# A two-layer decoder trunk in split precision: the high and low part of the activations in one 512-wide product

## The chip, the cores and the metric

One core of a Trainium2 chip runs the whole trunk in one launch. The metric is the device time in microseconds (us) of the program, as the median of several runs. The engines are TensorE (PE, matrix products), VectorE (DVE), ScalarE (ACT), GpSimd (POOL) and SyncE (SP, which issues the transfers here).

## The reference

The input x has 256 positions of width 1024. Two layers follow each other; each computes, with `rms_norm` and three token mixers in parallel:

```python
z = rms_norm(x, mix_g)            # projected to 7960 columns: z, xbc, dt, rq, rk, rv, rg, gq, gk, gv, gr, gates
...
x = x + out(sum of gate_b * branch_b(mixer_b))      # Mamba-2 SSD, retention, gated linear attention
h = rms_norm(x, ffn_g)
u = causal_dwconv(h @ w_up, w, b)                   # 2 x 2816 columns, 3 taps over positions
x = x + (silu(u[..., :2816]) * u[..., 2816:]) @ w_down
```

A last `rms_norm` closes the trunk. Everything is float32.

## The kernel before, in words

A float32 operand is split into a high part in the reduced format fp32r, which PE multiplies, and a low part, the rest. A product is the sum of three: high by high, high by low, low by high. T is the 256 positions.

**Weights.** SP streams pieces of 128 x 1024 from HBM into `raw` (four buffers), ACT casts each to `whi` (L183), DVE subtracts to get `wlo` (L184); `piece()` asks for pieces five ahead of their use. There are 300 such casts on each engine, scattered through their queues.

**Activations.** Each of three `slots` holds a normalized or activated operand, transposed, as two tiles: `slot_h` (high) and `slot_l` (low), 128 x n x 256.

**Two kinds of product.** *Token-major* products (`tok_major`, L274 to L276) hold activations as the stationary operand and stream 512 weight columns; they need two accumulators, one per 128 positions. *Channel-major* products (`chan_steps`, L227 to L229) hold 128 weight columns and stream the 256 positions: for each of 8 row blocks k and 2 halves j three products of width 256, high by high, high by low, low by high, all into the same half of one accumulator. `chan_two` interleaves two such products, `chan_major` makes one. They are used for xbc (3 of them), rq, rk (2 each), gq, gk, and for the 22 column pairs of the up projection: 31 in a layer. `narrow` (L256, L260) is a short product for the small columns.

**PSUM.** `mm_tile` gives the accumulators of these products: 512 columns, one bank, four of them in rotation. `mx_tile` gives four more for everything else, among them the four sums of the down projection.

**Order at the start of a layer.** `chan_two` makes xbc 2 and xbc 0, then `chan_major` xbc 1, then comes the narrow group, then z, then two gates, then rq, rk and so on. As a channel product ends, its result goes to `take_xbc`: DVE multiplies it by the norm's factors `r_bc` into a `tm` tile (L459), ACT (L463) and DVE (six steps of L466) convolve it, ACT takes a tanh (L470), DVE multiplies (L471). `take_small` scales the narrow group's result (L475). `r_bc` itself comes at the end of `norm.factor` (a copy on ACT, L324). For the retention, a table `phases` is loaded over SP (L683) into `r_a` and multiplied by `r_bc` (L689).

**FFN.** `activate` takes an up product: DVE by `r_bc` (L1007), ACT and DVE convolve (L1012, L1014), ACT Silu (L1016), DVE multiplies the halves (L1017), ACT casts the high part (L1018), DVE makes the low part (L1019) in slot 2. `add_down` (L1024 to L1026) adds the down products of step j - 3 after the up product of step j; the last of them follow at the end.

Every engine takes its instructions in the order in which the program issues them; a scheduler of the framework sets that order when the program is built, and the waits between engines are fixed with it.

Of the kernel before, what the change touches and what calls it, by code (L numbers as in the profile page):

```python
# [17 lines left out]
P = 128  # L18
D = 1024
T = 256  # L20
# [107 lines left out]
def hybrid_trunk(ctx: ExitStack, tc: tile.TileContext, xT_in, x_in, wall, par, wa2, cst, phase, dret, fin, gbias, out):  # L128
# [27 lines left out]

    slots = []
    for i, n in enumerate((KT, KT, 4)):
        h = cpool.tile([P, n, T], F32R, name=f"slot_h{i}")
        lo = cpool.tile([P, n, T], F32R, name=f"slot_l{i}")  # L160
        slots.append((h, lo))


    loaded = {}
# [28 lines left out]
        return (a[:, c] for a in piece(p + o // step))  # L193

    def mm_tile():
        return ps.tile([P, 512], F32, name="mm", tag="mm", bufs=4)

    def mx_tile():
        return ps.tile([P, 512], F32, name="mx", tag="mx", bufs=4)
# [10 lines left out]
    def two(a):  # L210
        return a.rearrange("p (j t) -> p j t", j=2)
# [2 lines left out]
        return r_bc.unsqueeze(1).to_broadcast([P, 2, T])  # L214


    def chan_steps(l, kind, idx, act, acc, ks, nk=KT, cols=256, width=256, col0=0):

        ah, al = act
        nj = width // P  # L220
        for k in ks:
            wh, wl = weight(l, kind, idx, k, cols)
            for j in range(nj):
                c = slice(col0 + j * P, col0 + (j + 1) * P)
                o = acc[:, j * T:(j + 1) * T]
                first, last = k == 0 and j == 0, k == nk - 1 and j == nj - 1
                nc.tensor.matmul(o, lhsT=wh[:, c], rhs=ah[:, k, :], start=first, stop=False)  # L227
                nc.tensor.matmul(o, lhsT=wh[:, c], rhs=al[:, k, :], start=False, stop=False)  # L228
                nc.tensor.matmul(o, lhsT=wl[:, c], rhs=ah[:, k, :], start=False, stop=last)  # L229

    def chan_major(l, kind, idx, act, nk=KT, **more):
        acc = mm_tile()
        for k in range(0, nk, 2):
            chan_steps(l, kind, idx, act, acc, (k, k + 1), nk, **more)
            if k < nk - 2:
                yield
        return acc

    def chan_two(l, kind, idx, act, take):

        acc = [mm_tile() for _ in range(2)]
        for n in LATE:
            i, k = n // 8, n % 8
            chan_steps(l, kind, idx[i], act, acc[i], (k, k + 1))
            if k == KT - 2:
                take(idx[i], acc[i])
            yield

    def narrow(l, act):

        ah, al = act
        acc = mm_tile()
        both = piece(PIECE_AT[l, "small", 0][0])[0].rearrange("p (k c) -> p k c", c=P)
        for k in range(KT):
            def low():
                nc.tensor.matmul(acc[:64, :T], lhsT=both[:, k, :64], rhs=al[:, k, :], start=False, stop=False)  # L256

            if k == KT - 1:
                low()
            nc.tensor.matmul(acc[:, :T], lhsT=both[:, k, :], rhs=ah[:, k, :], start=(k == 0), stop=(k == KT - 1))  # L260
            if k < KT - 1:
                low()
        return acc

    def tok_major(l, kind, act, chunk=0, nk=KT):

        ah, al = act
        acc = [mm_tile() for _ in range(2)]
        for k in range(nk):
            wh, wl = weight(l, kind, chunk + k // 4, k % 4, 512)  # L270
            for t in range(2):
                c = slice(t * P, (t + 1) * P)
                first, last = k == 0, k == nk - 1
                nc.tensor.matmul(acc[t], lhsT=ah[:, k, c], rhs=wh, start=first, stop=False)  # L274
                nc.tensor.matmul(acc[t], lhsT=ah[:, k, c], rhs=wl, start=False, stop=False)  # L275
                nc.tensor.matmul(acc[t], lhsT=al[:, k, c], rhs=wh, start=False, stop=last)  # L276
            if k < nk - 1:
                yield
        return acc
# [150 lines left out]
    class Mixers:  # L430
# [3 lines left out]
        def __init__(self, l, norm):  # L434
            self.l, self.norm = l, norm
            self.pr = params[l]
            self.half = sm.tile([P, 30], F32, name="half", tag="half")
            nc.gpsimd.tensor_scalar(self.half[:, 0:30], self.pr[:, PO["conv_w"]:PO["conv_w"] + 30], 0.5, None,
                                    ALU.mult)
            self.aneg = sm.tile([P, 8], F32, name="aneg", tag="aneg")  # L440
            nc.scalar.activation(self.aneg, self.pc("a_log", 0, 8), AF.Exp)
            nc.vector.tensor_scalar(self.aneg, self.aneg, -1.0, None, ALU.mult)
            self.wa = mix.tile([P, T], F32, name="wa", tag="wa")
            nc.gpsimd.memset(self.wa, 0.0)
            for o in (32, 96):
                nc.sync.dma_start(self.wa[o:o + 16, :], wa2[l])
            y_h, y_l = slots[1]
            self.y_dst = [(y_h[:, 0:4, :], y_l[:, 0:4, :]), (y_h[:, 4:8, :], y_l[:, 4:8, :]), slots[2]]

        def pc(self, name, i=0, n=1):  # L450
            return self.pr[:, PO[name] + i:PO[name] + i + n]
# [2 lines left out]
        def take_xbc(self, b, acc):  # L454
            half = self.half
            if not hasattr(self, "xbc"):
                self.xbc = mix.tile([P, 6, T], F32, name="xbc", tag="g_work")
            ub = t_main()
            nc.vector.tensor_tensor(two(ub), two(acc), bc2(self.norm.r_bc), ALU.mult)  # L459
            for j in range(2):  # L460
                ct = 2 * b + j
                u, x = ub[:, j * T:(j + 1) * T], self.xbc[:, ct, :]
                nc.scalar.activation(x, u, AF.Identity, scale=half[:, 4 * ct + 3:4 * ct + 4],  # L463
                                     bias=half[:, 24 + ct:25 + ct])
                for d in (1, 2, 3):
                    nc.vector.scalar_tensor_tensor(x[:, d:], u[:, :T - d], half[:, 4 * ct + 3 - d:4 * ct + 4 - d],  # L466
                                                   x[:, d:], ALU.mult, ALU.add)
            th = t_main()
            xf = self.xbc[:, 2 * b:2 * b + 2, :]
            nc.scalar.activation(two(th), xf, AF.Tanh)  # L470
            nc.vector.scalar_tensor_tensor(xf, two(th), 1.0, xf, ALU.add, ALU.mult)  # L471
# [47 lines left out]
        def turn(self, h, wait):  # L519

            yield wait
            for q in (2 * h, 2 * h + 1):
                pt = mx_tile()
                for j in range(2):
                    for t in range(2):
                        c = (2 * q + j) * P
                        nc.tensor.transpose(pt[:, j * T + t * P:j * T + (t + 1) * P], self.merged[t][:, c:c + P], ident)
                mh, ml = (a[:, 2 * q:2 * q + 2, :].rearrange("p k t -> p (k t)") for a in slots[0])
                nc.scalar.activation(mh, pt, AF.Copy, scale=0.5)
                nc.vector.scalar_tensor_tensor(ml, pt, 0.5, mh.bitcast(F32), ALU.mult, ALU.subtract)  # L530
                yield 1


        def branch_operand(self, y, g, dst):

            h, lo = dst
            for c2 in range(2):
                pt = mx_tile()
                for j in range(2):
                    for t in range(2):  # L540
                        c = (2 * c2 + j) * P
                        nc.tensor.transpose(pt[:, j * T + t * P:j * T + (t + 1) * P], y[t][:, c:c + P], ident)  # L542
                for j in range(2):
                    ct = 2 * c2 + j
                    split_scaled(h[:, ct, :], lo[:, ct, :], pt[:, j * T:(j + 1) * T], self.pc(g, ct))
                yield 1
# [359 lines left out]
    def layer(l, norm):  # L906
# [92 lines left out]


        fx = slots[1]
        ah, al = slots[2]
        dacc = []

        def activate(j, acc):
            ub = t_main()
            nc.vector.tensor_tensor(two(ub), two(acc), bc2(norm.r_bc), ALU.mult)  # L1007
            cv = t_main()
            for i in range(2):
                ct = j + NF * i  # L1010
                u, a = ub[:, i * T:(i + 1) * T], cv[:, i * T:(i + 1) * T]
                nc.scalar.activation(a, u, AF.Identity, scale=mx.pc("fconv_w", 3 * ct + 2), bias=mx.pc("fconv_b", ct))  # L1012
                for d in (1, 2):
                    nc.vector.scalar_tensor_tensor(a[:, d:], u[:, :T - d], mx.pc("fconv_w", 3 * ct + 2 - d),  # L1014
                                                   a[:, d:], ALU.mult, ALU.add)
            nc.scalar.activation(cv[:, :T], cv[:, :T], AF.Silu)  # L1016
            nc.vector.tensor_tensor(cv[:, :T], cv[:, :T], cv[:, T:], ALU.mult)  # L1017
            nc.scalar.copy(ah[:, j % 4, :], cv[:, :T])  # L1018
            nc.vector.tensor_tensor(al[:, j % 4, :], cv[:, :T], ah[:, j % 4, :].bitcast(F32), ALU.subtract)  # L1019
# [186 lines left out]
```

## Time and profile before

| | |
|---|---|
| median of 3 runs | 933.4 us (932.29 to 935.02) |
| the profiled execution | 932.3 us, of which the span is 930.5 us |
| mean granted clock of PE | 0.994 of full speed |
| PE busy | 914.5 us (98%), 5726 products |
| DVE busy | 712.9 us (77%) |
| ACT busy | 506.8 us (54%) |
| mean traffic | 183 GB/s |

The span is the time between the first and the last recorded instruction; 1.8 us lie around it. Durations of PE's products overlap, since the next one enters the array before the last has left it; their starts are the better measure. A row that ends in a bracket tells how long its engine was idle before it, and which engine and line ended that.

### The profile page before, as it was taken

The page shows a single profiled execution, that of the slowest core. Times are in us where ns is not written, and L with a number is a line of the kernel's source. Part 1 is how long each engine was busy: PE and PEld are TensorE (multiplying, and loading weights), DVE is VectorE, ACT ScalarE, POOL GpSimd, SP SyncE. Part 2 cuts the span into 40 slices and gives each one's busy share as a digit, 9 for nine tenths or more (in the row PEclk, how much of TensorE's full clock was granted, in tenths as well). Part 3 has the DMA queues.
Part 4 walks back from the last instruction along what each step waited for, and adds up shares of the span by engine and source line. Part 5 has one row for each costly group of instructions (what it writes and reads, how often), then busy time and mean ns, then how long its engine had stood idle before and what let it go on. Part 6 is the DMA issues. An engine that isn't in the chain of part 4 may idle for free.

```text
span 930.5 us, 14996 instructions
## 1 busy us (share of the span) xinstructions
PE 914.5 (98%) x5726; PEld 816.1 (88%) x5726; DVE 712.9 (77%) x1111; ACT 506.8 (54%) x748; POOL 78.4 (8%) x74
## 2 busy tenths in 40 slices
PE   8999999999999999999999999999999999999995
PEld 7879889888889999999898898888888999999994
DVE  6976888576768887787799578777667697777775
ACT  6765454454456555555566635554545575555552
POOL 3032200003200000000002131000120000000001
PEclk9999999999999999999999999999999999999998
DMA  7775655556655656555466556444665566555531
GB/s 255 276 243 166 219 172 170 152 162 210 201 181 161 202 183 186 188 192 181 147 186 183 198 168 218 158 139 156 206 212 194 169 188 189 190 183 184 183 109 46
DMA packets 51288, 169.94 MB, mean 183 GB/s; under 512 B 5968, under 2 KB 8336, under 8 KB 51088
## 3 DMA queue, kind: packets, MB, share of 16 engines
q1 hardware_dynamic: 50928, 168.46, 56.3%
q8 instruction: 45, 0.74, 0.3%
q10 hardware_dynamic: 288, 0.52, 0.2%
q14 instruction: 27, 0.22, 0.1%
HBM read 165.81 MB, written 1.05 MB: 179 GB/s over the span
## 4 chain that ended last, share of the span: by engine, by line
PE 94%; DVE 3%; ACT 1%; DMA 1%; issue 0%; SPq 0%; ACTq 0%
PE mm L227 13%; PE mm L228 13%; PE mm L229 13%; PE mm L274 12%; PE mm L275 12%; PE mm L276 12%; PE mx L1025 4%; PE mx L1024 4%; PE mx L1026 4%; PE mx L555 2%; DVE wlo L184 1%; PE mx L558 1%; DVE xbc L466 1%; PE mx L542 1%; DMA x_t<-x_t 1%; PE mx L726 1%
## 5 line engine op out<-in xcount | busy, mean ns | idle before, releaser
L184 DVE TENSOR_TENSOR wlo<-raw,whi 128x1024 fp32r<-128x1024 f32 (+1 forms) x300 | 377.6, 1261 | 123.6 <-ACT whi L183 120.6
L183 ACT CAST whi<-raw 128x1024 fp32r<-128x1024 f32 (+1 forms) x302 | 311.7, 1034 | 266.4 <-PE mm L276 109.3
L227 PE MATMUL mm<-slot_h,whi 128*128 128x256 f32 x992 | 282.4, 285 | 2.2 <-ACT slot_h L302 2.2
L228 PE MATMUL mm<-slot_l,whi 128*128 128x256 f32 x992 | 281.5, 284 | 0.1
L229 PE MATMUL mm<-slot_h,wlo 128*128 128x256 f32 x992 | 281.5, 284 | 0.0
L274 PE MATMUL mm<-whi,slot_h 128*128 128x512 f32 x512 | 203.9, 398 | 0.0
L275 PE MATMUL mm<-wlo,slot_h 128*128 128x512 f32 x512 | 200.4, 391 | 0.0
L276 PE MATMUL mm<-whi,slot_l 128*128 128x512 f32 x512 | 200.3, 391 | 0.0
L227 PEld LDWEIGHTS mm<-slot_h,whi 128*128 128x128 f32 x992 | 190.5, 192 | 4.9 <-ACT slot_h L302 2.6
L228 PEld LDWEIGHTS mm<-slot_l,whi 128*128 128x128 f32 x992 | 190.7, 192 | 2.1 <-DVE slot_l L303 0.3
L229 PEld LDWEIGHTS mm<-slot_h,wlo 128*128 128x128 f32 x992 | 190.7, 192 | 0.1
L274 PEld LDWEIGHTS mm<-whi,slot_h 128*128 128x128 f32 x512 | 96.2, 188 | 20.6 <-issue 0.7
L276 PEld LDWEIGHTS mm<-whi,slot_l 128*128 128x128 f32 x512 | 96.1, 188 | 20.3
L275 PEld LDWEIGHTS mm<-wlo,slot_h 128*128 128x128 f32 x512 | 96.3, 188 | 18.7
L1014 DVE SCALAR_TENSOR_TENSOR tm<-tm,par 128x255 f32<-128x255 f32 (+1 forms) x176 | 73.6, 478 | 0.7 <-ACT tm L1012 0.7
L1024 PE MATMUL mx<-whi,slot_h 128*128 128x512 f32 x176 | 69.1, 392 | 0.0
L1025 PE MATMUL mx<-wlo,slot_h 128*128 128x512 f32 x176 | 69.0, 392 | 0.0
L1026 PE MATMUL mx<-whi,slot_l 128*128 128x512 f32 x176 | 68.5, 389 | 0.0
L1012 ACT ACTIVATE tm<-tm,par 128x256 f32<-128x256 f32 x88 | 48.0, 592 | 4.3 <-DVE tm L1007 4.3
L1007 DVE TENSOR_TENSOR tm<-mm,r_bc 128x512 f32<-128x512 f32 x44 | 30.4, 690 | 23.1 <-PE mm L229 23.1
L1018 ACT CAST slot_h<-tm 128x256 fp32r<-128x256 f32 x44 | 17.9, 406 | 49.1 <-DVE tm L1017 49.0
L1026 PEld LDWEIGHTS mx<-whi,slot_l 128*128 128x128 f32 x176 | 33.1, 188 | 7.1
(193 smaller groups left out, 758.6 us busy)
## 6 DMA issues: line engine op xcount, KB each, us to landing
raw<-w_all SPq DMA_DIRECT2D x292, 512.0 KB, 3.5
gate_b<-gate_b SPq DMA_DIRECT2D x12, 256.0 KB, 3.5
st<-ret_decay SPq DMA_DIRECT2D x8, 384.0 KB, 3.8
raw<-w_all SPq DMA_DIRECT2D x10, 256.0 KB, 3.9
x_t<-x_t SPq DMA_DIRECT2D x4, 256.0 KB, 5.8
xt<-x_tok SPq DMA_DIRECT2D x1, 1024.0 KB, 6.3
r_c<-q SPq DMA_DIRECT2D x16, 64.0 KB, 2.0
r_d<-q SPq DMA_DIRECT2D x16, 64.0 KB, 2.0
```

The costliest lines, as they stand in the source:

```text
L183: nc.scalar.copy(h_out, r_in)
L184: nc.vector.tensor_tensor(l_out, r_in, h_out.bitcast(F32), ALU.subtract)
L227: nc.tensor.matmul(o, lhsT=wh[:, c], rhs=ah[:, k, :], start=first, stop=False)
L228: nc.tensor.matmul(o, lhsT=wh[:, c], rhs=al[:, k, :], start=False, stop=False)
L229: nc.tensor.matmul(o, lhsT=wl[:, c], rhs=ah[:, k, :], start=False, stop=last)
L274: nc.tensor.matmul(acc[t], lhsT=ah[:, k, c], rhs=wh, start=first, stop=False)
L275: nc.tensor.matmul(acc[t], lhsT=ah[:, k, c], rhs=wl, start=False, stop=False)
L276: nc.tensor.matmul(acc[t], lhsT=al[:, k, c], rhs=wh, start=False, stop=last)
L1014: nc.vector.scalar_tensor_tensor(a[:, d:], u[:, :T - d], mx.pc("fconv_w", 3 * ct + 2 - d), a[:, d:], ALU.mult, ALU.add)
L1024: nc.tensor.matmul(o, lhsT=ah[:, a, tok], rhs=wh, start=first, stop=False)
L1025: nc.tensor.matmul(o, lhsT=ah[:, a, tok], rhs=wl, start=False, stop=False)
L1026: nc.tensor.matmul(o, lhsT=al[:, a, tok], rhs=wh, start=False, stop=last)
```

## The change

The two tiles of a slot become one, with the high and the low part of a row block side by side. A channel product then issues two products per weight block instead of three: the high weights stream both parts in one 512-wide product into a whole bank, the low weights stream the high part into its first half. A channel accumulator so has two banks, one for each j, and each bank's two halves have to be added: `joined` copies the second halves to a `tm` tile on ACT and adds the first halves on DVE, ahead of what was done with the accumulator before. `mm_tile` becomes a pair of banks, two pairs in rotation. A token-major product uses the two banks of a pair as its two accumulators; the narrow group takes a pair and uses half a bank. In `take_xbc` and `activate` the multiplication by `r_bc` works in place on the joined tile.

```diff
-        h = cpool.tile([P, n, T], F32R, name=f"slot_h{i}")
-        lo = cpool.tile([P, n, T], F32R, name=f"slot_l{i}")
-        slots.append((h, lo))
+        both = cpool.tile([P, n, 2, T], F32R, name=f"slot{i}")
+        slots.append((both[:, :, 0, :], both[:, :, 1, :], both))
...
     def mm_tile():
-        return ps.tile([P, 512], F32, name="mm", tag="mm", bufs=4)
+        return ps.tile([P, 2, 512], F32, name="mm", tag="mm", bufs=2)
...
-    def chan_steps(l, kind, idx, act, acc, ks, nk=KT, cols=256, width=256, col0=0):
+    def chan_steps(l, kind, idx, act, acc, ks, nk=KT):
...
-                nc.tensor.matmul(o, lhsT=wh[:, c], rhs=ah[:, k, :], start=first, stop=False)
-                nc.tensor.matmul(o, lhsT=wh[:, c], rhs=al[:, k, :], start=False, stop=False)
-                nc.tensor.matmul(o, lhsT=wl[:, c], rhs=ah[:, k, :], start=False, stop=last)
+                nc.tensor.matmul(acc[:, j, :], lhsT=wh[:, c], rhs=both[:, k], start=(k == 0), stop=False)
+                nc.tensor.matmul(acc[:, j, :T], lhsT=wl[:, c], rhs=ah[:, k, :], start=False, stop=(k == nk - 1))
+
+    def joined(acc):
+
+        u = t_main()
+        nc.scalar.copy(two(u), acc[:, :, T:])
+        nc.vector.tensor_tensor(two(u), acc[:, :, :T], two(u), ALU.add)
+        return u
...
-        return acc
+        return joined(acc)
...
-                take(idx[i], acc[i])
+                take(idx[i], joined(acc[i]))
...
     def narrow(l, act):
-        acc = mm_tile()
+        acc = mm_tile()[:, 0, :]
...
     def tok_major(l, kind, act, chunk=0, nk=KT):
-        acc = [mm_tile() for _ in range(2)]
+        pair = mm_tile()
+        acc = [pair[:, t, :] for t in range(2)]
...
         def activate(j, acc):
-            ub = t_main()
+            ub = acc
```

The lines of the changed kernel that the text names: cast L182, weight low part L183, the pair of products L224 and L225, the copy L230, the join L231, narrow group L259 and L263, token-major L278 to L280, xbc L462 (before L459), L466 (L463), L469 (L466), L473 (L470), L474 (L471), small L478 (L475), r_a L692 (L689), phases L686 (L683), FFN L1010 (L1007) and L1022 (L1019).

The scheduler places the new instructions, and others shift with them. DVE's queue at the start of layer 0, from the weight cast next to the first xbc's scaling; before (tm_334 is xbc 2's scaled result, wlo pieces of weights, mm_169 the accumulator of xbc 0):

```order
L184 TENSOR_TENSOR wlo_279<-raw_277,whi_278 128x1024
L459 TENSOR_TENSOR tm_334<-mm_168,r_bc_331 128x512
L184 TENSOR_TENSOR wlo_349<-raw_347,whi_348 128x1024
L466 SCALAR_TENSOR_TENSOR xbc_333<-tm_334,half_159,xbc_333 128x255 x2
L466 SCALAR_TENSOR_TENSOR xbc_333<-tm_334,half_159,xbc_333 128x254 x2
L466 SCALAR_TENSOR_TENSOR xbc_333<-tm_334,half_159,xbc_333 128x253 x2
L184 TENSOR_TENSOR wlo_381<-raw_379,whi_380 128x1024
L471 SCALAR_TENSOR_TENSOR xbc_333<-tm_344,xbc_333 128x512
L459 TENSOR_TENSOR tm_365<-mm_169,r_bc_331 128x512
```

and now (tm_276 belongs to xbc 2, tm_332 to xbc 0):

```order
L183 TENSOR_TENSOR wlo_320<-raw_318,whi_319 128x1024
L462 TENSOR_TENSOR tm_276<-tm_276,r_bc_303 128x512
L183 TENSOR_TENSOR wlo_350<-raw_348,whi_349 128x1024
L469 SCALAR_TENSOR_TENSOR xbc_305<-tm_276,half_156,xbc_305 128x255 x2
L469 SCALAR_TENSOR_TENSOR xbc_305<-tm_276,half_156,xbc_305 128x254 x2
L469 SCALAR_TENSOR_TENSOR xbc_305<-tm_276,half_156,xbc_305 128x253 x2
L183 TENSOR_TENSOR wlo_372<-raw_370,whi_371 128x1024
L474 SCALAR_TENSOR_TENSOR xbc_305<-tm_315,xbc_305 128x512
L231 TENSOR_TENSOR tm_332<-mm_166,tm_332 128x512
L183 TENSOR_TENSOR wlo_410<-raw_408,whi_409 128x1024
L462 TENSOR_TENSOR tm_332<-tm_332,r_bc_303 128x512
L692 TENSOR_TENSOR r_a_761<-r_a_761,r_bc_303 128x512
```

The scaling of xbc 0 (tm_365, now tm_332) has its join and one more weight cast ahead of it, and the multiplication of `r_a`, which stood elsewhere, follows it.

PE's queue from xbc 1's last products through the narrow group to z, with the engines whose signal is waited for, before (mm_378 is xbc 1, mm_452 the narrow group, mm_477 z):

```order
L227 MATMUL mm_378<-slot_h0_87,whi_228 128x256
L228 MATMUL mm_378<-slot_l0_88,whi_228 128x256
L229 MATMUL mm_378<-slot_h0_87,wlo_229 128x256
L260 MATMUL mm_452<-slot_h0_87,whi_246 128x256 [waits Activation_49]
L256 MATMUL mm_452<-slot_l0_88,whi_246 64x256
...
L260 MATMUL mm_452<-slot_h0_87,whi_246 128x256
L274 MATMUL mm_477<-whi_278,slot_h0_87 128x512 [waits DVE_49,PE_49]
L275 MATMUL mm_477<-wlo_279,slot_h0_87 128x512
```

and now (mm_347, mm_407, mm_432):

```order
L326 MATMUL mx_301<-dg_298,ones_79 128x256 [waits DVE_49]
L225 MATMUL mm_347<-slot0_87,wlo_218 128x256
L224 MATMUL mm_347<-slot0_87,whi_217 128x512
L225 MATMUL mm_347<-slot0_87,wlo_218 128x256
L263 MATMUL mm_407<-slot0_87,whi_231 128x256 [waits DVE_49,PE_49]
L259 MATMUL mm_407<-slot0_87,whi_231 64x256
...
L263 MATMUL mm_407<-slot0_87,whi_231 128x256
L278 MATMUL mm_432<-whi_255,slot0_87 128x512 [waits DVE_49]
```

The narrow group used to wait for its weights from ACT and now waits for DVE: its accumulator is the pair of xbc 0, which the join L231 of tm_332 frees. z waits for DVE too: its pair was the narrow group's, and L478 frees it, which stands on DVE behind L692 and five of the six L469 of tm_332.

SP's queue around the table for the retention, before:

```order
L494 DMA gate_b_590<-gate_b 128x512
L176 DMA raw_379<-w_all 128x1024
L176 DMA raw_409<-w_all 128x1024
L176 DMA raw_453<-w_all 128x1024
L176 DMA raw_479<-w_all 128x1024
L683 DMA r_a_809<-phases 128x512
L176 DMA raw_497<-w_all 128x1024
L1078 DMA xt_73<-x_tok 128x2048
```

and now:

```order
L497 DMA gate_b_544<-gate_b 128x512
L175 DMA raw_348<-w_all 128x1024
L175 DMA raw_370<-w_all 128x1024
L175 DMA raw_408<-w_all 128x1024
L175 DMA raw_433<-w_all 128x1024
L175 DMA raw_451<-w_all 128x1024
L686 DMA r_a_761<-phases 128x512
L1081 DMA xt_73<-x_tok 128x2048
```

The load of `r_a` stands behind one more weight piece of 128 x 1024.

## Rows read from the trace of the kernel before

**Rows 1.** Page, part 1: busy us, share of the span, instructions, by engine

```profile
PE 914.5 (98%) x5726; PEld 816.1 (88%) x5726; DVE 712.9 (77%) x1111; ACT 506.8 (54%) x748; POOL 78.4 (8%) x74
```

**Rows 2.** Timeline of PE in layer 0's FFN: start us, own us, line, operation

```profile
353.88 0.28 PE L228 MATMUL mm<-slot_l,whi 128*128 128x256 f32 x1
...
356.88 0.28 PE L229 MATMUL mm<-slot_h,wlo 128*128 128x256 f32 x1
```

**Rows 3.** Timeline of PE, token-major products of layer 1's mixers

```profile
704.24 0.39 PE L274 MATMUL mm<-whi,slot_h 128*128 128x512 f32 x1
...
710.36 0.39 PE L274 MATMUL mm<-whi,slot_h 128*128 128x512 f32 x1
```

**Rows 4.** ACT's groups by line: count, then busy us, mean ns, idle before

```profile
L590 ACT COPY sg_c<-mx 128x512 f32<-128x512 f32 x4 | 2.3, 580 | 0.0
```

**Rows 5.** Timeline of DVE in layer 0's FFN, in brackets idle us and releaser

```profile
296.44 0.68 DVE L1007 TENSOR_TENSOR tm<-mm,r_bc 128x512 f32<-128x512 f32 x1
...
301.56 0.68 DVE L1007 TENSOR_TENSOR tm<-mm,r_bc 128x512 f32<-128x512 f32 x1
...
359.72 0.69 DVE L1007 TENSOR_TENSOR tm<-mm,r_bc 128x512 f32<-128x512 f32 x1 [0.46 <-PE mm L229]
```

**Rows 6.** Timeline of DVE at the start of layer 0

```profile
26.21 0.69 DVE L459 TENSOR_TENSOR tm<-mm,r_bc 128x512 f32<-128x512 f32 x1 [0.16 <-ACT r_bc L324]
...
28.30 2.45 DVE L466 SCALAR_TENSOR_TENSOR xbc<-tm,half,xbc 128x255 f32<-128x255 f32 x6
...
31.80 0.68 DVE L471 SCALAR_TENSOR_TENSOR xbc<-tm,xbc 128x512 f32<-128x512 f32 x1
32.40 0.68 DVE L459 TENSOR_TENSOR tm<-mm,r_bc 128x512 f32<-128x512 f32 x1
...
37.64 0.41 DVE L475 TENSOR_TENSOR small<-mm,r_bc 128x256 f32<-128x256 f32 x1
```

**Rows 7.** Timeline of PE, layer 0: narrow group, z, first rq product

```profile
27.52 0.28 PE L260 MATMUL mm<-slot_h,whi 128*128 128x256 f32 x1
...
29.38 0.40 PE L274 MATMUL mm<-whi,slot_h 128*128 128x512 f32 x1
...
67.81 0.28 PE L227 MATMUL mm<-slot_h,whi 128*128 128x256 f32 x1
```

**Rows 8.** Timeline of SP's queue; view of DMA issues: count, KB each, us to landing

```profile
28.79 0.42 SPq L683 DMA_DIRECT2D r_a<-phases  x1
...
r_a<-phases SPq DMA_DIRECT2D x2, 256.0 KB, 3.9
```

**Rows 9.** Timeline of PE, layer 1: xbc 1, narrow group, z, first rq product

```profile
478.07 0.28 PE L227 MATMUL mm<-slot_h,whi 128*128 128x256 f32 x1
...
483.83 0.28 PE L260 MATMUL mm<-slot_h,whi 128*128 128x256 f32 x1
...
485.70 0.40 PE L274 MATMUL mm<-whi,slot_h 128*128 128x512 f32 x1
...
522.72 0.28 PE L227 MATMUL mm<-slot_h,whi 128*128 128x256 f32 x1
```

**Rows 10.** Timeline of ACT at the start of layer 1

```profile
483.91 1.05 ACT L183 CAST whi<-raw 128x1024 fp32r<-128x1024 f32 x1 [1.26 <-PE mm L228]
```

**Rows 11.** Timelines of ACT and PE, start of layer 0's FFN

```profile
287.14 1.05 ACT L183 CAST whi<-raw 128x1024 fp32r<-128x1024 f32 x1 [0.94 <-PE mm L228]
...
288.86 0.28 PE L227 MATMUL mm<-slot_h,whi 128*128 128x256 f32 x1
```

**Rows 12.** Timelines of DVE and PE, end of layer 1's FFN

```profile
912.39 0.43 DVE L1019 TENSOR_TENSOR slot_l<-tm,slot_h 128x256 fp32r<-128x256 f32 x1 [0.47 <-ACT slot_h L1018]
...
913.38 0.39 PE L1024 MATMUL mx<-whi,slot_h 128*128 128x512 f32 x1
```

**Rows 13.** Windows at the start: us; busy (count) PE, PEld, DVE, ACT, POOL; granted clock; DMA

```profile
8.00:10.00 2.00, 2.00 (x10) 2.00 (x11) 1.98 (x5) 2.00 (x5) 0.00 (x0) 0.50 1.00 381
10.00:12.00 2.00, 2.00 (x13) 2.00 (x13) 1.79 (x4) 2.00 (x6) 0.00 (x0) 0.64 0.79 225
```

More of the change, by code (lines that the diff above doesn't have):

```diff
@@ L214, in bc2, with chan_major @@
         return r_bc.unsqueeze(1).to_broadcast([P, 2, T])
-    def chan_steps(l, kind, idx, act, acc, ks, nk=KT, cols=256, width=256, col0=0):
-        ah, al = act
-        nj = width // P
+    def chan_steps(l, kind, idx, act, acc, ks, nk=KT):
+        ah, _, both = act
         for k in ks:
[L222 to L226, printed above, removed]
-                nc.tensor.matmul(o, lhsT=wh[:, c], rhs=ah[:, k, :], start=first, stop=False)
-                nc.tensor.matmul(o, lhsT=wh[:, c], rhs=al[:, k, :], start=False, stop=False)
-                nc.tensor.matmul(o, lhsT=wl[:, c], rhs=ah[:, k, :], start=False, stop=last)
-    def chan_major(l, kind, idx, act, nk=KT, **more):
+            wh, wl = weight(l, kind, idx, k, 256)
+            for j in range(2):
+                c = slice(j * P, (j + 1) * P)
+                nc.tensor.matmul(acc[:, j, :], lhsT=wh[:, c], rhs=both[:, k], start=(k == 0), stop=False)
[5 more added lines that the diff above has]
+        return u
+    def chan_major(l, kind, idx, act, nk=KT):
         acc = mm_tile()
         for k in range(0, nk, 2):
-            chan_steps(l, kind, idx, act, acc, (k, k + 1), nk, **more)
+            chan_steps(l, kind, idx, act, acc, (k, k + 1), nk)
             if k < nk - 2:
                 yield
-        return acc
+        return joined(acc)
     def chan_two(l, kind, idx, act, take):
@@ L245, in chan_two @@
             if k == KT - 2:
-                take(idx[i], acc[i])
+                take(idx[i], joined(acc[i]))
             yield
     def narrow(l, act):
-        ah, al = act
-        acc = mm_tile()
+        ah, al, _ = act
+        acc = mm_tile()[:, 0, :]
         both = piece(PIECE_AT[l, "small", 0][0])[0].rearrange("p (k c) -> p k c", c=P)
@@ L265, in tok_major @@
     def tok_major(l, kind, act, chunk=0, nk=KT):
-        ah, al = act
-        acc = [mm_tile() for _ in range(2)]
+        ah, al, _ = act
+        pair = mm_tile()
+        acc = [pair[:, t, :] for t in range(2)]
         for k in range(nk):
@@ L446, in __init__ @@
                 nc.sync.dma_start(self.wa[o:o + 16, :], wa2[l])
-            y_h, y_l = slots[1]
-            self.y_dst = [(y_h[:, 0:4, :], y_l[:, 0:4, :]), (y_h[:, 4:8, :], y_l[:, 4:8, :]), slots[2]]
+            self.y_dst = [tuple(a[:, o:o + 4] for a in slots[1]) for o in (0, 4)] + [slots[2]]
         def pc(self, name, i=0, n=1):
@@ L527, in turn @@
                         nc.tensor.transpose(pt[:, j * T + t * P:j * T + (t + 1) * P], self.merged[t][:, c:c + P], ident)
-                mh, ml = (a[:, 2 * q:2 * q + 2, :].rearrange("p k t -> p (k t)") for a in slots[0])
-                nc.scalar.activation(mh, pt, AF.Copy, scale=0.5)
-                nc.vector.scalar_tensor_tensor(ml, pt, 0.5, mh.bitcast(F32), ALU.mult, ALU.subtract)
+                mh, ml = (a[:, 2 * q:2 * q + 2, :] for a in slots[0][:2])
+                nc.scalar.activation(mh, two(pt), AF.Copy, scale=0.5)
+                nc.vector.scalar_tensor_tensor(ml, two(pt), 0.5, mh.bitcast(F32), ALU.mult, ALU.subtract)
                 yield 1
         def branch_operand(self, y, g, dst):
-            h, lo = dst
+            h, lo, _ = dst
             for c2 in range(2):
@@ L1001, in layer @@
         fx = slots[1]
-        ah, al = slots[2]
+        ah, al, _ = slots[2]
         dacc = []
         def activate(j, acc):
-            ub = t_main()
+            ub = acc
             nc.vector.tensor_tensor(two(ub), two(acc), bc2(norm.r_bc), ALU.mult)
```

## The prediction

> **What bounds the kernel now.** I read the busy times first, then TensorE's timeline, then the queues of VectorE and ScalarE at the places where a new wait can arise. TensorE (PE) is busy in 98% of the span, VectorE (DVE) in 77%, ScalarE (ACT) in 54% [rows 1]. So the time is the sum of PE's products, and any gap that the change opens on PE adds to it in full. A product's own duration overlaps with the next one; its price is the distance between starts. Twenty-five steps of 256-wide products take 356.88 - 353.88 = 3.00 us, 0.120 us each [rows 2]. Twenty-seven steps of 512-wide ones take 710.36 - 704.24 = 6.12 us, 0.2267 us each [rows 3]. Twice the width costs less than twice the time: each product carries about 2 x 0.120 - 0.2267 = 0.0133 us that does not grow with its width.
>
> **What the change removes.** The 62 channel products of the two layers issue 16 triples each: 992 times L227, L228 and L229. In each triple the first two become one 512-wide product. 992 x 0.0133 = **13.2 us less** on PE, all of it on the path. The rows leave little doubt about the size: both widths run at steady pace for dozens of steps, and the weight loads are part of both intervals. The Trainium skill, "TensorE: Matmul & The Clock Gate", section "Back-to-back issue gap", gives an isolated gap of N/2.4 ns plus 2.5 ns, by which a merged pair would save 2.5 ns and the whole change 2.5 us. The trace disagrees: 120 and 226.7 ns are both 13 ns above N/2.4, and the measurement decides.
>
> **What it adds.** Each of the 62 channel products is now closed by an ACT copy of the two second halves (128x512 out of PSUM) and a DVE addition of the same size. The nearest rows: a PSUM copy of this size on ACT takes 0.58 us [rows 4]; a 128x512 DVE operation with a PSUM operand starts its successor after 0.60 us (31.80 to 32.40) and lasts 0.69 us [rows 6]. That is 36 us more on ACT and 37 to 43 us more on DVE. In steady state PE hides it. In the long FFN stretch PE needs 16 pairs and 12 products of the down projection per step: 16 x 0.3467 + 12 x 0.2267 = 8.27 us (before: 8.48). Where DVE ran without pause, one step with two weight casts took 301.56 - 296.44 = 5.12 us; the third cast adds some 1.1 and the addition 0.60, so 6.8 us. DVE waits for PE there, not the reverse (the 0.46 us before L1007) [rows 5]. I cost the joins in the FFN's steady part at nothing; if that cover were gone, the price would be the excess of DVE's step over 8.27 us, some 38 times.
>
> **What it moves: the accumulators.** Four single banks, free one by one, become two pairs. A third user now waits for the first pair to be joined, and the join stands in DVE's queue. Two narrow users (the 16-product L260/L256 group and the token-major z) take a whole pair each. This bites where channel products follow one another fast, at the start of a layer.
>
> *Layer 0.* PE reaches the narrow group at 27.52, z at 29.38 [rows 7]; with some 32 pairs at 0.0133 us done before it that is about 27.1. The narrow group needs the pair of xbc 0, so it waits for that join (L231). Before it on DVE stand the first normalization L462 (before L459), a cast, six convolution steps, a cast and L474. L459 started at 26.21 because r_bc had just arrived; now one cast more stands before r_bc's copy on ACT, and a cast and a join on DVE: I take 28.1. From L459 to L471 the row shows 31.80 - 26.21 = 5.59 us, L471 takes 0.60, the join 0.69: 28.1 + 5.59 + 0.60 + 0.69 = 35.0. PE stands still for 35.0 - 27.1 = **7.9 us**. The narrow group takes 29.38 - 27.52 = 1.86 us and ends at 36.9. Then z waits for L478 (before L475, at 37.64), which frees the narrow group's pair. It has a cast, L462, L692 and five convolution steps before it: 35.0 + 1.1 + 0.6 + 0.6 + 2.0 + 0.4 = 39.7. L692 itself waits for the phases table. That DMA was issued at 28.79 and lands in 3.9 us [rows 8]; it now stands one weight load later in SP's queue, and its raw buffers come free later, so 38 or so, which puts z at 41. I take 40.2, a stall of **3.3 us**. PE may win some back: from z to the next channel product it needed 67.81 - 29.38 = 38.4 us, in layer 1 for the same work 522.72 - 485.70 = 37.0 [rows 7, 9], so 1.4 us of slack. Layer 0: 7.9 + 3.3 - 1.4 = **+9.8 us** (bounds: 5 if the phases come in time and L462 is not late, 13 if the load queue slips further).
>
> *Layer 1.* Xbc 1 started at 478.07, the narrow group at 483.83, z at 485.70 [rows 9]. Xbc 1 takes the pair of xbc 2, whose join follows the last product by an ACT cast, a copy, a DVE cast and the addition, and is over at about 479.7: a stall of 2.0 us against 477.7. Xbc 1 takes 16 x 0.3467 = 5.55 us. The join of xbc 0 stands on DVE behind a cast of a weight piece, whose ACT part can start only when xbc 1's last product has freed the buffer, as the cast at 483.91 does now [rows 10]. So the narrow group waits for 1.0 (ACT cast) + 1.1 (DVE cast) + 0.60 (L474) + 0.69 (join) = 3.4, with hand-overs **3.6 us**. After it z waits for L462, six convolution steps (one ACT step of some 0.5 us ahead, 2.45 us [rows 6]) and L478 at 0.4: 4.1 us after the join, of which the narrow group covers 1.86: **2.2 us**. Layer 1: 2.0 + 3.6 + 2.2 = **+7.8 us**, bounds 3 and 9; the stretch behind shows no slack I can count on.
>
> *Start of the FFN, twice.* up 2 needs the pair of up 0. It started at 288.86 [rows 11]; now PE is free at 288.86 - 32 x 0.0133 = 288.4. ACT has the cast (287.14, started 0.2 earlier) ahead of the copy, so the copy ends at 288.5; DVE then has a cast of 1.1 us before the addition: 289.9. 1.5 us each, **+3.1 us**. up 3 has the time of up 2 in addition and should not wait.
>
> *End of layer 1.* The last activation ended at 912.39 + 0.43 = 912.82, and PE asks for it at 913.38 [rows 12]. Copy and addition put some 1.2 us ahead of it, the products end at the same distance: **+0.5 us**. The other two-bank users (rk, rv, gv) wait for joins that lie a full product (5.55 us) back; at nothing.
>
> **The clock.** After PE's standstill at the start of the kernel the granted clock was 0.50 between 8 and 10 us and 0.64 between 10 and 12 [rows 13], so 10 and 13 products where 2 / 0.12 = 16.7 fit: 10.4 x 0.12 = 1.25 us lost. I count that once for layer 0's long stall (1.3) and half of it for layer 1 (0.7).
>
> **Sum.** -13.2 + 9.8 + 7.8 + 3.1 + 0.5 + 1.3 + 0.7 = +10.0 us. The profiled execution took 932.3 us (span 930.5); 942.3. The median of the three runs is 1.1 us above it, so 933.4 + 10 = **943 us**.
>
> **Rivals.**
> *The joins come in time (faster).* If at the two layer starts the join of xbc 0 is over before PE asks for the narrow group (27.1 and 485.2), the stalls there vanish with their clock loss: 933.4 - 13.2 + 3.1 + 0.5 = 924 us. That needs 8 us less in DVE's queue in layer 0; for it speaks only that DVE is idle in a quarter of the span, against it that the queue has a fixed order and 5.6 us of other work in it. 0.14. If only one of the two starts is absorbed, about 932 or 935: 0.12, two thirds of it within what cannot be told.
> *DVE sets the FFN's pace (slower still).* DVE's step is 6.8 us of work, so it decides the pace once more than 8.27 - 6.8 = 1.5 us of its waits for ACT stay in the chain; before, its waits were 8.48 - 6.2 = 2.3 us. If 0.2 to 0.8 us of excess remained, 38 steps would cost 8 to 30 us: 951 to 973. 0.08.
> *The fixed part is not saved.* If a 512-wide product past the same weights cost twice a 256-wide one, nothing is gained and the stalls stay: 956. The 512-wide rows [rows 3] speak against it, though their stationary operand is an activation and not a weight. 0.05. By the 2.5 ns of the Trainium skill's page "TensorE: Matmul & The Clock Gate", section "Back-to-back issue gap", it would be 954.
> The forecast itself: 0.61.
>
> **How the numbers follow.** A difference under 0.3% (2.8 us: 930.6 to 936.2) is about what a measurement of this kernel can't tell from none. Faster: the first rival and a part of the half-absorbed one, 0.16. Same: 0.12. Slower: 0.72. The bounds of the stalls alone (layer 0 5 to 13, layer 1 3 to 9) put the forecast's own range at 933 to 949. To hold eight in ten with the half-absorbed case and part of the DVE case, it goes from 929 to 955.
>
> **Signs.** Right: starts 0.227 us after an L224 and 0.120 after an L225; PE idle of some 8 us before L263 and 3 us before L278 in layer 0, 2, 4 and 2 us in layer 1, and 1.5 us before the third up product, with DVE named as releaser; FFN step 8.27 us; DVE about 755 us. Wrong: no idle time before L263, or idle time of PE in every FFN step, or a pair that takes 0.36 us as three narrow products did.

## The result: 964 us, slower by 3.3%

The changed kernel took a median of 964.34 us in four runs (960.33 to 966.19), the kernel before 932.89 us beside it. The ratio is 1.0327, with a 95% interval of 1.029 to 1.0364. The forecast was 943 us, slower by 10 us, with a range that ended at 955: the sign was right, the size a third of what came.

The page of the changed kernel, its first lines:

```profile
span 962.3 us, 13103 instructions
## 1 busy us (share of the span) xinstructions
PE 920.3 (96%) x4734; PEld 769.9 (80%) x4734; DVE 751.8 (78%) x1173; ACT 538.5 (56%) x810; POOL 76.7 (8%) x74
```

992 products fewer than in [rows 1], as forecast, and DVE at 752 us (forecast about 755). But PE is busy for 920 us where 914.5 less the gain should stand. The waits of PE (engine, line and what it waited for, us in total, times, longest):

```profile
PE mm L263 <- DVE tm L231: 12.2, 2, 8.6
PE mm L224 <- DVE tm L231: 4.5, 3, 1.5
PE mm L278 <- DVE small L478: 2.9, 2, 1.6
PE mx L545 <- DVE tx L565: 2.9, 1, 2.9
PE mx L545 <- DMA raw<-w_all: 2.8, 1, 2.8
```

The first three are the places that the forecast named. The last two are not: L545 transposes the SSM's output in each layer (before: L542, which did not wait). The view puts the second of them down to a DMA; the timeline shows PE resuming at 126.89 as L565, which makes the operand, passes its first half (it starts at 126.15 and two of them take 1.29 us).

All waits of this view add up to 30.1 us, against 4.1 before; the span less PE's busy time grew by the same 26.0 us (42.0 against 16.0). The rest of the loss is in the clock. Windows of 2 us around the stall before L545 in layer 0 (us, then busy time and count of PE, PEld, DVE, ACT and POOL, granted clock of PE, DMA share, GB/s):

```profile
122.00:124.00 2.00, 2.00 (x10) 1.43 (x8) 1.97 (x7) 1.05 (x1) 0.03 (x1) 1.00 0.95 389
124.00:126.00 2.00, 0.12 (x1) 0.00 (x0) 1.93 (x3) 1.04 (x1) 1.90 (x1) 1.00 0.74 211
126.00:128.00 2.00, 1.11 (x5) 0.60 (x6) 1.97 (x4) 0.00 (x0) 0.00 (x0) 0.95 0.20 82
128.00:130.00 2.00, 2.00 (x10) 1.58 (x11) 2.00 (x3) 0.95 (x2) 0.00 (x0) 0.50 0.23 37
130.00:132.00 2.00, 2.00 (x8) 1.49 (x6) 2.00 (x6) 0.86 (x2) 0.00 (x0) 0.50 0.82 281
132.00:134.00 2.00, 2.00 (x6) 1.62 (x5) 0.20 (x1) 0.00 (x0) 0.00 (x0) 0.50 0.54 207
134.00:136.00 2.00, 2.00 (x9) 1.56 (x9) 0.00 (x0) 0.25 (x1) 0.00 (x0) 0.84 0.00 0
```

PE stands still for some 2.8 us, and then works for almost 7 us at 1.2 GHz (granted clock 0.50): this stall cost its length and about as much again. Taking the granted clock over the whole run in windows of 1 us, and counting 1 minus the clock for the time in which PE was busy, the low level cost 11.2 us, against 1.7 before. PE counts as busy all the while, which is why its busy time went up.

The steady part of the FFN gained less than forecast. PE's timeline in an FFN step of the changed kernel:

```profile
361.95 0.39 PE L224 MATMUL mm<-slot,whi 128*128 128x512 f32 x1
362.18 0.28 PE L225 MATMUL mm<-slot,wlo 128*128 128x256 f32 x1
362.29 0.40 PE L224 MATMUL mm<-slot,whi 128*128 128x512 f32 x1
362.52 0.28 PE L225 MATMUL mm<-slot,wlo 128*128 128x256 f32 x1
...
370.34 0.39 PE L224 MATMUL mm<-slot,whi 128*128 128x512 f32 x1
```

The step takes 370.34 - 361.95 = 8.39 us, not 8.27. Its 16 pairs take 0.3525 us each (the median over 38 steps), where 0.2267 + 0.120 = 0.3467 was forecast: the saving per triple is 0.0075 us and not 0.0133, 7.4 us in all and not 13.2.

**The account.** Span +31.8 us: idle time of PE +26.0, slow clock +9.5, gain of the pairs -7.4; that is 28.1. The 26.0 hold every gap, so the other 3.7 us lie within PE's busy time, and what makes them is not shown: less the low clock, that time fell by only 3.7 us (+5.8 - 9.5). The 7.4 us are an estimate, the FFN's pace times 992.

### The profile page after: what moved, and what is told of

Its sections match the earlier page's. It is cut to its first block, busy times and chain, and to the rows that moved or that the text cites. A ratio compares the mean times of both kernels' runs of the same rounds, so it can differ in the third digit from the quotient of the medians.

```text
span 962.3 us, 13103 instructions
## 1 busy us (share of the span) xinstructions
PE 920.3 (96%) x4734; PEld 769.9 (80%) x4734; DVE 751.8 (78%) x1173; ACT 538.5 (56%) x810; POOL 76.7 (8%) x74
## 4 chain that ended last, share of the span: by engine, by line
PE 86%; DVE 7%; DMA 3%; ACT 2%; issue 1%; SPq 0%; ACTq 0%; DVEq 0%
PE mm L224 23%; PE mm L278 12%; PE mm L225 11%; PE mm L280 11%; PE mm L279 11%; PE mx L1027 4%; PE mx L1028 4%; PE mx L1029 4%; DVE wlo L183 2%; DMA raw<-w_all 1%; PE mx L558 1%; ACT whi L182 1%; PE mx L545 1%; DMA r_a<-phases 1%; PE mx L729 1%
## 5 line engine op out<-in xcount | busy, mean ns | idle before, releaser
L183 DVE TENSOR_TENSOR wlo<-raw,whi 128x1024 fp32r<-128x1024 f32 (+1 forms) x300 | 377.1, 1259 | 141.7 <-ACT whi L182 141.4
L182 ACT CAST whi<-raw 128x1024 fp32r<-128x1024 f32 (+1 forms) x302 | 312.3, 1035 | 272.5 <-PE mm L280 131.9
L224 PE MATMUL mm<-slot,whi 128*128 128x512 f32 x992 | 355.1, 400 | 6.5 <-DVE tm L231 4.5
L225 PE MATMUL mm<-slot,wlo 128*128 128x256 f32 x992 | 278.6, 281 | 0.0
L224 PEld LDWEIGHTS mm<-slot,whi 128*128 128x128 f32 x992 | 186.4, 188 | 53.4 <-DVE tm L231 5.7
L278 PE MATMUL mm<-whi,slot 128*128 128x512 f32 x512 | 206.4, 403 | 2.9 <-DVE small L478 2.9
L280 PE MATMUL mm<-whi,slot 128*128 128x512 f32 x512 | 202.1, 395 | 0.0
L279 PE MATMUL mm<-wlo,slot 128*128 128x512 f32 x512 | 202.0, 395 | 0.0
L225 PEld LDWEIGHTS mm<-slot,wlo 128*128 128x128 f32 x992 | 187.6, 189 | 2.3 <-DVE wlo L183 0.5
L278 PEld LDWEIGHTS mm<-whi,slot 128*128 128x128 f32 x512 | 97.6, 191 | 24.5 <-DVE small L478 3.4
L280 PEld LDWEIGHTS mm<-whi,slot 128*128 128x128 f32 x512 | 97.4, 190 | 21.1
L279 PEld LDWEIGHTS mm<-wlo,slot 128*128 128x128 f32 x512 | 97.6, 191 | 19.0
L1027 PE MATMUL mx<-whi,slot 128*128 128x512 f32 x176 | 69.2, 393 | 0.5 <-ACT slot L1021 0.5
L1028 PE MATMUL mx<-wlo,slot 128*128 128x512 f32 x176 | 69.0, 392 | 0.0
L1029 PE MATMUL mx<-whi,slot 128*128 128x512 f32 x176 | 68.6, 390 | 0.0
L231 DVE TENSOR_TENSOR tm<-mm,tm 128x512 f32<-128x512 f32 x62 | 42.5, 686 | 3.0 <-ACT tm L230 1.8
L230 ACT COPY tm<-mm 128x512 f32<-128x512 f32 x62 | 35.8, 578 | 1.8 <-PE mm L225 1.8
```

The source lines that it names most:

```text
L182: nc.scalar.copy(h_out, r_in)
L183: nc.vector.tensor_tensor(l_out, r_in, h_out.bitcast(F32), ALU.subtract)
L224: nc.tensor.matmul(acc[:, j, :], lhsT=wh[:, c], rhs=both[:, k], start=(k == 0), stop=False)
L225: nc.tensor.matmul(acc[:, j, :T], lhsT=wl[:, c], rhs=ah[:, k, :], start=False, stop=(k == nk - 1))
L1027: nc.tensor.matmul(o, lhsT=ah[:, a, tok], rhs=wh, start=first, stop=False)
L1028: nc.tensor.matmul(o, lhsT=ah[:, a, tok], rhs=wl, start=False, stop=False)
```

## Experiments

Theory: three separate losses. The accumulators that come free late stall the layer starts; the joins of rq and rk make DVE late for the SSM's output; the clock falls behind each such stall. Rivals: only the number of banks counts; the late layer start is what makes the SSM late; the new layout itself costs; the wide product is worth nothing. All times are medians, with the ratio to runs of the kernel before on the same chip. These runs had medians of 932.9 to 934.2 us from set to set, so a difference between kernels of different sets carries a further microsecond of doubt.

**Xbc products without the change.**

```diff
-        acc = [mm_tile() for _ in range(2)]
+        pair = mm_tile()
+        acc = [pair[:, i, :] for i in range(2)]
...
-            chan_steps(l, kind, idx[i], act, acc[i], (k, k + 1))
+            (chan_thin if thin else chan_steps)(l, kind, idx[i], act, acc[i], (k, k + 1))
```

`chan_thin` is the old loop of three 256-wide products; xbc 1 and the narrow group take the two banks of the other pair.

> Only the three xbc products of each layer go back to three 256-wide products in one bank without a join: xbc 2 and xbc 0 in the two banks of one pair, xbc 1 and the narrow group in the two of the other. Theory: the stalls at the two layer starts are the pair rotation's and go; between the milestones they and the clock after them cost 10.3 us in layer 0 and 10.9 in layer 1, against 0.7 us of lost gain: 943.8 us, and PE has no idle time before L263 or its successor. If the stall of the SSM transposes in each layer (6.6 and 6.9 us with the slow clock behind it) is a consequence of the late layer start, it goes too: 930. Rival: the extra ACT and DVE work of the joins of rq and rk is what makes the transposes late: then that stall stays, 944. Rival two: the layer starts are late for another reason (the order on DVE): above 955.

Measured: 955.6 us, ratio 1.0228 (1.0195 to 1.0261). The theory's number was missed by 12 us. PE's waits show why: the narrow group, now behind z's first products, waits only 0.5 us, but z waits, 4.6 us of it in layer 0, and xbc 1 waits 1.2 us there for the same line L479.

```profile
PE mm L295 <- DVE tm L479: 5.0, 2, 4.6
PE mm L224 <- DVE tm L244: 3.0, 2, 1.5
PE mx L562 <- DMA raw<-w_all: 2.8, 1, 2.8
PE mx L562 <- DVE tx L582: 2.8, 1, 2.8
```

L295 is z, L479 the scaling of the xbc results. In the kernel before, z worked through most of its first accumulator, from 29.38 on, while the second was still taken until L459 ended at 33.08 [rows 6, 7]; a pair comes free only as a whole. The stalls before the transposes (now L562) stay as they were.

**The first two up products as well.**

> As the kernel with three-product xbc, and the first two up products of each layer too, so that every interleaved pair of products shares a pair of accumulators without a join. Theory: the wait of the third up product for the join of the first (1.5 us in each layer) goes, 0.5 us of gain is lost: 2.5 us less than the kernel with three-product xbc alone. Rival: the wait turns into one for L1010 of the first up product and stays: no difference, or 0.5 us more.

Measured: 951.89 us, 1.0196 (1.0176 to 1.0215), 3.7 us less than without. The wait of L224 for the join, 3.0 us in the two layers, is gone from the view, so the stalls that the forecast put at 3.1 us were real. The times alone don't show it: the two intervals overlap, and the four runs without this edit lie between 950.87 and 957.17.

**The wide product undone, all else kept.**

```diff
-                nc.tensor.matmul(acc[:, j, :], lhsT=wh[:, c], rhs=both[:, k], start=(k == 0), stop=False)
+                nc.tensor.matmul(acc[:, j, :T], lhsT=wh[:, c], rhs=both[:, k, 0], start=(k == 0), stop=False)
+                nc.tensor.matmul(acc[:, j, T:], lhsT=wh[:, c], rhs=both[:, k, 1], start=False, stop=False)
```

> Everything of the change stays (pairs, joins, layout), but the 512-wide product is issued as two of 256, high part into the first half, low part into the second. Theory from the trace of the changed kernel: a pair takes 0.3525 us there and three products 0.360, so 992 x 0.0075 = 7.4 us more than the changed kernel where PE sets the pace: 972 us. The forecast's price (0.0133 each) would give 13.2 us, 977. Rival: the pair is worth nothing, 964.

Measured: 970.71 us, 1.0397 (1.0375 to 1.0418): 6.4 us above the changed kernel. The intervals leave some 4 us of doubt on it. It fits the 7.4 us from the trace, not the forecast's 13.2, and not nothing.

**Two wide, then two narrow.**

> The changed kernel with the products of a weight block in another order: the 512-wide ones of both halves, then the 256-wide ones of both. Rival A: a 512-wide product costs 0.009 us more because a 256-wide one follows it; then only one in two pays, and a pair of pairs takes some 0.699 instead of 0.705 us: about 3 us less, 961. Rival B: the extra belongs to this product whatever follows: no change, 964.

Measured: 959.04 us, 1.027 (1.0242 to 1.0298), 5.3 us less than the changed kernel. The kernel with the same order in up 2 to 21 alone (below) shows it in PE's timeline of an FFN step, two products of a kind in one row:

```profile
343.58 0.62 PE L227 MATMUL mm<-slot,whi 128*128 128x512 f32 x2
344.04 0.40 PE L230 MATMUL mm<-slot,wlo 128*128 128x256 f32 x2
344.27 0.63 PE L227 MATMUL mm<-slot,whi 128*128 128x512 f32 x2
...
348.45 0.63 PE L227 MATMUL mm<-slot,whi 128*128 128x512 f32 x2
```

(348.45 - 343.58) / 14 = 0.348 us a pair. So most of the missing 0.0058 us belongs to the alternation of the two widths: 992 x 0.0045 = 4.5 us. The rest of the 5.3 us can be shorter waits: in the profiled executions the span less PE's busy time is 39.7 us, against 42.0.

**Wide only in up 2 to 21, on single banks.**

```diff
-        return ps.tile([P, 2, 512], F32, name="mm", tag="mm", bufs=2)
+        return ps.tile([P, 512], F32, name="mm", tag="mm", bufs=4)
...
+        for j in range(2):
+            o = u[:, j * T:(j + 1) * T]
+            nc.scalar.copy(o, acc[j][:, T:])
+            nc.vector.tensor_tensor(o, acc[j][:, :T], o, ALU.add)
```

> The wide product only for up 2 to up 21 of each layer (40 of 62 products); all others are three 256-wide products without a join. The accumulators are four single banks again, a wide product takes two of them, and its two halves are copied and added bank by bank. Theory: the mixers are then as before the change, no stall of PE at the layer starts nor before the SSM transposes; the gain is 40 x 16 x 0.0075 = 4.8 us: 928 us. Rival: joins bank by bank make ACT or DVE late in the FFN, or the third up product waits: 933 or more. Rival two: the slot's new layout itself slows the mixers (a stall before the transposes remains, 6.6 us a layer): 940.

Measured: 930.13 us, 0.996 (0.9942 to 0.9978): faster than before by 3 us, 2 us short of the theory's number. No wait of PE above 1.3 us is left, and the clock cost nothing in the profiled execution.

**The same with the grouped order.**

> As the kernel with the wide product in up 2 to 21 alone on single banks, with the two 512-wide products of a weight block issued before the two 256-wide ones. The grouped order gave 5.3 us over 62 products; over 40 it should give 3.4 us more: 925 us. Rival: the 5.3 us came out of shorter stalls at the layer starts, not from the pace in the FFN: 928, as without it.

Measured: 927.75 us, 0.9934 (0.9911 to 0.9957), the best version found, 0.7% faster than before. The step from 930.13 is 2.4 us where 3.4 were expected; the intervals overlap. The longest waits of PE that are left stood in the kernel before too (there 1.1 and 0.8 us):

```profile
PE mx L1090 <- POOL ones L150: 1.1, 1, 1.1
PE mx L618 <- DVE da L609: 0.7, 1, 0.7
```

**Single banks, only xbc in three products.**

> Single banks, only the xbc products as three 256-wide ones; rq, rk, gq, gk and all up products wide and joined. Theory: what stalls PE at the layer starts is that a pair comes free only as a whole, which the kernel with three-product xbc on pairs kept; with single banks z can begin on one bank: no idle time there, about 10 us less than that kernel for the starts. If the joins of rq and rk on DVE make the SSM transposes late, that stall (2.8 us and the slow clock, 6.7 a layer) stays: 941 us. If it was the pairs too, it goes: 929.

Measured: 942.86 us, 1.0097 (1.0071 to 1.0123), 12.7 us less than the same on pairs. The waits of z and xbc 1 are gone, those before the transposes (here L565) are not:

```profile
PE mx L565 <- DVE tx L585: 5.5, 2, 2.8
PE mm L227 <- DVE tm L249: 3.0, 2, 1.5
PE mx L616 <- DVE da L607: 2.2, 1, 2.2
```

So the SSM's lateness does not come from the layer start. (L616 waited 0.8 us in the kernel before.) The clock behind these two stalls was not the same: in layer 1 it stayed low for 10 us, in layer 0, from 116.65 to 119.41, PE stood still for 2.76 us and kept its clock:

```profile
116.00:118.00 2.00, 0.65 (x3) 0.19 (x2) 1.93 (x3) 0.00 (x0) 1.82 (x1) 1.00 0.94 365
120.00:122.00 2.00, 2.00 (x14) 1.44 (x14) 1.85 (x2) 1.83 (x3) 0.00 (x0) 1.00 0.03 8
```

**The whole change on single banks.**

> The whole change, with single banks in place of pairs: every channel product wide, on two single banks, joined bank by bank. Theory: two wide products in flight use all four banks either way, so the narrow group and z still wait for joins, but can begin on a bank as it comes free: part of the 21 us of the layer starts goes, 950 to 958. Rival A: only the number of banks counts: no change, 964. Rival B: only the granularity counts: 943.

Measured: 958.97 us, 1.0274 (1.025 to 1.0297), 5.4 us less than on pairs and a microsecond above the expected stretch. The two intervals just touch. z no longer waits, the narrow group still does (11.2 us in the two layers): with every channel product wide, four single banks don't remove that wait.

**Wide rq and rk added to the fast kernel.**

```diff
-            a = yield from chan_major(l, kind, 0, x_act, bank=mm_tile())
+            a = yield from chan_major(l, kind, 0, x_act)
```

(and the same for b; `bank` selects the three-product form)

> The kernel with the wide product in up 2 to 21 on single banks, and rq and rk (four products a layer) wide and joined as well. Theory: the joins of rq and rk, and s = tm x r_a reading the joined tile from SBUF beside GpSimd, put the SSM's last steps later in DVE's queue; PE waits 2.8 us a layer before the SSM transposes, and the granted clock falls behind that: 12 us more than without, 942. Rival: it was the joins of gq and gk or the two wide up products at the start: 930, as without, and no idle time of PE before the transposes.

Measured: 940.97 us, 1.0074 (1.0059 to 1.009), 10.8 us above the kernel with up 2 to 21 alone. The two stalls are back, and with them the low clock, 8.5 us by the count above, 6.8 of them right behind the two stalls:

```profile
PE mx L565 <- DVE tx L585: 5.5, 2, 2.8
```

Eight joined products in the two layers, which gain 1.0 us by their pace, cost 11.

**The layout alone.**

> No wide product at all: the change's slot layout, with high and low part side by side, and every channel product as three 256-wide ones in one of four single banks, as before the change. Theory: the layout costs and gives nothing: 933, PE's FFN step 8.50 us, and the 3 us of the kernel with wide up products come from the wide products. Rival: part of those 3 us come from another order of the instructions at the start (no slow clock there): 930 to 931.

Measured: 933.99 us, 1.0003 (0.9992 to 1.0014). The layout is free, and the gain of the fast kernels is the wide product's: runs with the same mean clock of 0.996 took 933.2 and 933.4 us here, 929.1 and 929.4 with the wide up products.

## Why the prediction was wrong

**Right: the places and lengths of the forecast stalls.** The narrow group was forecast to stall 7.9 us in layer 0 and 3.6 in layer 1. In the changed kernel's timeline of PE the brackets say 8.57 and 3.62:

```profile
35.92 0.55 PE L263 MATMUL mm<-slot,whi 128*128 128x256 f32 x1 [8.57 <-DVE tm L231]
...
41.10 0.50 PE L278 MATMUL mm<-whi,slot 128*128 128x512 f32 x1 [1.63 <-DVE small L478]
```

```profile
496.32 0.50 PE L224 MATMUL mm<-slot,whi 128*128 128x512 f32 x1 [1.50 <-DVE tm L231]
505.86 0.35 PE L263 MATMUL mm<-slot,whi 128*128 128x256 f32 x1 [3.62 <-DVE tm L231]
510.20 0.80 PE L278 MATMUL mm<-whi,slot 128*128 128x512 f32 x1 [1.30 <-DVE small L478]
```

z started at 41.1 (the forecast took 40.2, with 41 as what the late phases table would give), and its stalls are shorter than 3.3 and 2.2 because the narrow group itself ran at the low clock. Xbc 1 in layer 1 stalled 1.50 us (2.0 forecast), up 2 1.5 (1.5). With the end of layer 1 these terms were 22.6 us, gross, and came to 20.1. The 1.4 us of slack in layer 0 were there too: from z to the next channel product it is 37.05 us, where it was 38.4. That DVE's step stays below PE's in the FFN held as well: no wait of PE in its steady part.

**Wrong, first: "The other two-bank users ... at nothing".** That step looked at rk, rv and gv as users of an accumulator, and costed the joins of rq and rk at nothing because PE had slack for the bank. It did not follow who is queued behind the joins on DVE: the SSM's last steps, and these had no time to spare already. DVE and then PE in the kernel before, from the last rotary product to the transposes:

```profile
97.80 0.68 DVE L698 TENSOR_TENSOR s<-mm,r_a 128x512 f32<-128x512 f32 x1
...
99.73 0.69 DVE L667 TENSOR_TENSOR tx<-mx,sg_c 128x512 f32<-128x512 f32 x1
...
110.78 1.28 DVE L562 TENSOR_TENSOR tx<-tx,rs_y 128x512 f32<-128x512 f32 x2
```

```profile
111.52 0.44 PE L542 MATMUL mx<-cs,tx 128*128 128x128 f32 x2
```

The first of the two L562 was over some 0.1 us before PE read it. DVE in the changed kernel behind the last rotary product:

```profile
108.53 0.68 DVE L231 TENSOR_TENSOR tm<-mm,tm 128x512 f32<-128x512 f32 x1
109.25 0.69 DVE L701 TENSOR_TENSOR s<-tm,r_a 128x512 f32<-128x512 f32 x1
109.86 0.69 DVE L700 TENSOR_TENSOR q<-tm,r_a 128x512 f32<-128x512 f32 x1
110.47 1.79 DVE L701 TENSOR_TENSOR s<-tm,r_a 128x512 f32<-128x512 f32 x1
112.18 0.68 DVE L670 TENSOR_TENSOR tx<-mx,sg_c 128x512 f32<-128x512 f32 x1
```

From the next product's start on PE (rv, 106.23) to L670 it is 5.95 us; before, 99.73 - 96.40 = 3.33. Up to the operand itself, L565, it is 126.15 - 106.23 = 19.92 us; before, 110.78 - 96.40 = 14.38. Of these 5.5 us more, PE covers 2.8 with 12 more token-major products that now stand ahead of L545, and stands still for the rest.

The joins are not all of the 5.5 us. The second L701 takes 1.1 us longer than the first beside an operation of GpSimd (last section), and close to L565 a small operation meets GpSimd again. DVE and GpSimd in the changed kernel:

```profile
124.17 1.75 DVE L292 SCALAR_TENSOR_TENSOR rs_a<-rs_a,rs_v 128x4 f32<-128x4 f32 x1
```

```profile
123.97 1.93 POOL L715 TENSOR_TENSOR r_b<-r_b,mean 128x1024 f32<-128x1024 f32 x1 [10.29 <-DVE rs_y L293]
```

L292 takes 0.16 us at its first turn (120.97), here 1.75: it ends as L715 does, 1.6 us late. In layer 1 it is L291, which takes 1.91 us. In the kernel before, this operation of GpSimd came after the SSM's last steps:

```profile
112.30 2.75 POOL L712 TENSOR_TENSOR r_b<-r_b,mean 128x1024 f32<-128x1024 f32 x1 [11.35 <-DVE mean L711]
```

The two waits make 2.7 of the 5.5 us, by these rows; the rest is the joins and weight casts that changed their place. Cost: two stalls of 2.8 us and the clock behind them. The kernel with wide rq and rk added shows that these products are the cause, 10.8 us for them alone; it has both waits for GpSimd too (1.78 and 1.75 us), so the shares of joins, order and GpSimd were not tried apart.

**Wrong, second: the clock, 1.3 + 0.7.** The forecast priced one recovery from the start of the kernel [rows 13] and counted it one and a half times. There were four: behind the two layer starts the low level cost 1.6 and 2.8 us, by the count above, and behind each of the two stalls before L545 3.4 us. That is 9.5 us more than before, 7.5 more than forecast, and most of it follows from the first step. The price was low as well: by the granted clock the stretch of [rows 13] cost 1.7 us and not 1.25.

**Wrong, third: the size of the gain.** The sum took the price of a 512-wide product from a stretch of nothing else [rows 3] and that of a 256-wide one from a stretch of nothing else [rows 2]. Alternating, they take 0.3525 us a pair. 7.4 us instead of 13.2: 5.8 us of the miss. The price with the wide product undone (6.4 us) and that of the grouped order (5.3 us) both bear it out. The Trainium skill's "TensorE: Matmul & The Clock Gate", section "Back-to-back issue gap", gives an isolated product 2.5 ns above its streaming time. The trace disagrees: the 7.5 ns saved per triple lie between that and the forecast's 13.3.

Together: 5.8 (gain) + 7.5 (clock) + 5.7 (L545), less 1.1 (the forecast's stalls, net of its 1.4 us of slack, were 21.2 against 20.1), plus 3.7 unassigned: 21.6 us of the 21.8 us between the forecast's +10.0 and the span's +31.8. The rival of a DVE-bound FFN, whose price would have reached the measured time, did not occur.

## What to carry to other kernels

A product that becomes faster on the bounding engine pays only where its extra work on the other engines has nobody waiting behind it: here the same edit gains 3 us in the long FFN loop and loses 11 us in eight rotary products, so try it loop by loop. Before costing added instructions at nothing, walk the queue they stand in to its next consumer on the bounding engine, look how close that consumer already runs, and what another engine runs beside it in the new order. Price a gap on TensorE at its length plus a recovery of the clock, as a range and not as one number, and price a mixed stream from a mixed stream.

## What the runs showed that was not expected

- A DVE operation whose two operands lie in SBUF waited for GpSimd, here and at L292 above. L701 in the fence above starts at 110.47 and takes 1.79 us. GpSimd's timeline in the changed kernel has:

```profile
110.09 1.61 POOL L702 TENSOR_TENSOR q<-q,s 128x512 f32<-128x512 f32 x1 [9.57 <-DMA st<-ret_decay]
```

  It ends at 111.70, 0.56 us before L701 does. The eight L701 take 0.691 to 1.787 us; before the change, with one operand in PSUM, the same eight (L698) took 0.681 to 0.692. The join moved the operand from PSUM into SBUF. The Trainium skill, "SBUF — State Buffer", section "SBUF: two separate sides", says that a DVE operation with two SBUF inputs and a GpSimd operation that reads SBUF exclude each other on a shared pair of ports; these rows agree.
- Two widths in alternation cost PE 0.0058 us a pair over the sum of their own rates; two of each in turn leave 0.0013. Why was not tried.
- The low clock behind a stall varied. Eight of these kernels stall some 2.8 us before the SSM's transposes in each layer; behind these 16 stalls PE worked for 0 to 10 us at the low clock, 5.7 us in the mean, of which half, 2.9 us, is lost. Behind the stalls of 1.5 us before up 2 there was none.
